# The first output pair's weight sums four units behind their fetch, and other cuts of the last stores, in a hybrid decoder layer

## The chip, the cores and the metric

The kernel runs on one core of one Trainium2 chip. The metric is the device time of one execution in microseconds (us). Three runs of the kernel before took 766.54, 766.78 and 766.79 us; the median is 766.78. Engines are named as in the profile: PE is TensorE with its matmuls, PEld its weight loads, DVE is VectorE, ACT ScalarE, POOL GpSimd, SP SyncE. PE, DVE and ACT each work through their own instructions in the order in which the built program lists them; SP, ACT and POOL also issue the transfers between device memory and on-chip memory.

## The reference

One decoder layer on 256 tokens (two token tiles of 128) of width 2048, in float32. A normed input goes through one wide projection. Two token mixers (a gated delta rule and a block attention, 8 heads of 128 each) give `oa` and `ob`; the end of the layer is:

```python
u_a = oa @ w_branch_a
u_b = ob @ w_branch_b
merged = jax.nn.sigmoid(gate_a) * u_a + jax.nn.sigmoid(gate_b) * u_b
y = merged @ w_out
out = x + rms_norm(y, post_norm_w)
```

`gate_a` and `gate_b` are 2048 columns each of the wide projection. The change touches the product with `w_out`, and the store of `out`.

## The kernel before

**Products in halves.** A float32 operand is split into a high part (cast on ACT, L241) and a low part (the difference, on DVE, L242), and a product is the sum of high by high, high by low and low by high. The tiles are named hi_x and lo_x for a product x. For every weight tile of 128 x 1024 there is thus one ACT cast and one DVE difference, and PE's second matmul of a group needs the low part. `proj_n` does this for a column block of 512: it loads four blocks of 128 rows at a time (raw, three buffers) and splits them in two pieces; lo_gb_1_1 is the low part of the second piece (u = 1) of the second load (kb = 1) of a gate_b block.

**Seven products instead of eight.** The branch products and half of the output product take column blocks in pairs, and multiply 2 x 2 blocks with seven products (`seven`). Three weight tiles tq[0], tq[1], tq[2] for that are fetched by POOL (`fetch`, L776) and added up on DVE (`weight_sums`, L784): first tq[0] += tq[2], in two halves of 128 x 1024, then tq[1] += tq[0], in two halves. After the first two sums POOL issues a fetch that accumulates into tq[2] (L787). `prepare` does the fetch and queues the sums; it is called four times, the last time for the first output pair, column blocks 0 and 1 of w_out. The sums' results are named tq_y there.

**Order of the work.** The program is written out as a stream of matmuls. After each group of six (in a projection with two token tiles) `tick` advances several queues of generators by half a unit; a generator says with `yield n` after how many units it wants to go on. `T_WAIT` has the units that each of the four `weight_sums` waits behind its `prepare`; within it, each half sum is followed by one unit. The instructions of matmuls and of the sums keep their program order; other instructions of an engine are placed by the framework's scheduler when the program is built.

Around the last `prepare` the program does: `merge` of merged column blocks 0 and 1 (transposes on PE, then L1256 to L1271 on ACT and DVE: the transposed blocks mT, the block sums sum_tt, sum_tw, sum_tv, sum_lo for the seven products), `branch(2)` (its weighting is L1168 to L1171 and L1219 to L1220 on DVE), gate_b's column block 3 (a_gb, hi_gb, lo_gb), and then the seven products of the first output pair (a_y, with a_ub of branch block 3 between them).

**The end.** `last` multiplies the last column blocks per token tile; `weigh` squares on ACT (L1316) and multiplies by the norm's weights on DVE (L1317); `finish` takes the root, the reciprocal (L1332), and scales and adds x in five column pieces on DVE (L1336), each stored by its own transfer (L1340): the first token tile's on SP, the last one's on SP and ACT in turn. The last instructions of all engines stand at L1436.

Of the kernel before, what the change touches and what calls it, by code (L numbers as in the profile page):

```python
# [15 lines left out]
P = 128  # L16
# [8 lines left out]
PGT_WAIT = 0.5  # L25
D_WAIT = 7
SC_WAIT = 4
T_WAIT = (5, 4, 4, 7)
L_WAIT = 5
LC_WAIT = 3.5  # L30
INV = (0.6, 2)
# [59 lines left out]
def hybrid_layer(  # L91
# [15 lines left out]
    nc = tc.nc  # L107
    B, S, D = x.shape
# [8 lines left out]
    of = out.rearrange("b s d -> (b s) d")  # L117
# [64 lines left out]
    for c in range(KT // 2):  # L182

        for t in range(NT):
            cs = slice(c * 256, (c + 1) * 256)
# [592 lines left out]
    def weight_sums(tq, w, c, wait):  # L778

        yield wait  # L780
        for o, a in ((0, 2), (1, 0)):
            for u in range(2):
                us = slice(2 * u, 2 * u + 2)
                pin(nc.vector.tensor_tensor(tq[o][:, us], tq[o][:, us], tq[a][:, us], op=ALU.add))  # L784
                yield 1
            if o == 0:
                nc.gpsimd.dma_start(tq[2], block(w, c, 1, 1), accum_op=ALU.add)  # L787
        formed.append(True)

    def prepare(tq, w, c, order):  # L790

        fetch(tq, w, c, order)
        formed.clear()
        sq.add(weight_sums(tq, w, c, T_WAIT[len(tqs)]))
        tqs.append(tq)
# [512 lines left out]
    yw = [big.tile([P, D], F32, tag=f"z{1 - t}", name=f"yw_{t}") for t in range(NT)]  # L1308
# [20 lines left out]
    def finish(t, rb):  # L1329
        rs = wk.tile([P, 1], F32, tag="rstd", name=f"rs_{t}")  # L1330
        pin(nc.scalar.activation(rs, ssy[t][:, 3:4], AF.Sqrt, bias=rb, scale=1.0 / D))
        pin(nc.vector.reciprocal(rs, rs))  # L1332
        for i, (c0, c1) in enumerate(((0, 256), (256, 768), (768, 1280), (1280, 1792), (1792, D))):
            cs = slice(c0, c1)
            pin(
                nc.vector.scalar_tensor_tensor(  # L1336
                    yw[t][:, cs], yw[t][:, cs], rs, hx[:, t, cs], op0=ALU.mult, op1=ALU.add
                )
            )
            (nc.sync if t == 0 or i % 2 == 0 else nc.scalar).dma_start(of[t * P : (t + 1) * P, cs], yw[t][:, cs])  # L1340

    def rest(c, h, pts):

# [60 lines left out]
    last(0, c12, 0, 512)  # L1404
    weigh(3, 0, c12)
    finish(0, rbs[0])
    last(1, c22[:, :256], 0, 256)
    weigh(3, 1, c22[:, :256], 0, 0, 256)
    rb = so_far(1, rbs[1])
    last(1, c22b[:, 256:], 256, 256)  # L1410
    weigh(3, 1, c22b[:, 256:], 3, 256, 256)
    finish(1, rb)


# [26 lines left out]
```

## Time and profile before

| | |
|---|---|
| profiled execution | 766.79 us, its span 765.1 us |
| PEld, ACT, POOL busy | 646.3, 452.7, 52.0 us |
| HBM read and written | 162.72 MB and 3.15 MB, mean 217 GB/s over the span |
| granted TensorE clock, mean over the span | 0.997 |
| sums L784 of the first output pair on DVE | four of 1.22 us, first start 646.0, last 653.4 us |
| the last token tile's stores, from issue to landing | 1.9 to 2.3 us each |

A row of a timeline has the start in us from the span's start, the duration, the engine, the line, the operation and its tiles; a bracket at its end gives the idle time before it and what ended that. Durations of consecutive instructions on one engine overlap a little, so that the distance of two starts, not the duration, says what one more instruction costs. The clock is that granted to TensorE, 1.00 at full speed.

### The profile page before, as it was taken

Reading aid. Unit: us, or ns where it says so; the run is one execution under the profiler, and the core shown is the slowest. Engines: PE = TensorE matmul, PEld = TensorE weight load, DVE = VectorE, ACT = ScalarE, POOL = GpSimd, SP = SyncE. Lnnn points to the kernel's source line nnn. Section 1 sums busy time; section 2 is a strip of 40 time slices with the busy share of each in tenths; the row PEclk is TensorE's granted clock in tenths of the full one; section 3 lists DMA queues with packets and bytes.
Section 4 is the critical chain, followed back from the end, with each engine's and each line's share of the span. In section 5 each row is a group of like instructions: output and inputs, shape, how many; then the busy total and the mean of one; then the engine's idle time right before and its main releaser. Section 6 shows DMA issues by size and latency. Waiting matters only on the chain.

```text
span 765.1 us, 10514 instructions
## 1 busy us (share of the span) xinstructions
PE 755.9 (99%) x3941; PEld 646.3 (84%) x3941; DVE 583.2 (76%) x944; ACT 452.7 (59%) x684; POOL 52.0 (7%) x78
## 2 busy tenths in 40 slices
PE   9999999999999999999999999999999999999996
PEld 8998988899888888888899888787888887888885
DVE  6877669885977898775457876678797778789764
ACT  6776666657655654554556475656556656565751
POOL 4000001112000000003001000101000100100000
PEclk9999999999999999999999999999999999999998
DMA  9585676458555557568437756798979775997972
GB/s 307 177 260 197 194 212 173 137 163 229 185 200 177 189 186 217 171 187 205 127 108 274 209 166 214 250 328 245 334 216 326 221 274 174 338 286 216 270 257 111
DMA packets 100665, 166.56 MB, mean 218 GB/s; under 512 B 3589, under 2 KB 49286, under 8 KB 100102
## 3 DMA queue, kind: packets, MB, share of 16 engines
q1 hardware_dynamic: 89526, 134.93, 53.9%
q0 software_dynamic: 10768, 30.42, 15.4%
q8 instruction: 31, 0.51, 0.3%
q10 hardware_dynamic: 320, 0.53, 0.2%
q14 instruction: 20, 0.16, 0.1%
HBM read 162.72 MB, written 3.15 MB: 217 GB/s over the span
## 4 chain that ended last, share of the span: by engine, by line
PE 94%; DVE 3%; ACT 2%; issue 0%; DVEq 0%
PE a_ga L163 11%; PE a_gb L163 10%; PE a_y L163 9%; PE a_ub L163 6%; PE a_zg L163 6%; PE a_mq L163 6%; PE a_v L163 6%; PE a_mk L163 6%; PE a_k L163 6%; PE a_zm L163 6%; PE a_mv L163 6%; PE a_q L163 4%; PE a_ua L163 4%; PE s L163 1%; PE ms L163 1%; PE po L163 1%
## 5 line engine op out<-in xcount | busy, mean ns | idle before, releaser
L163 PE MATMUL a_ga<-hi_ga,hT 128*128 128x512 f32 x256 | 82.1, 394 | 0.0
L163 PE MATMUL a_gb<-hi_gb,hT 128*128 128x512 f32 x256 | 81.0, 391 | 0.0
L163 PEld LDWEIGHTS a_gb<-hi_gb,hT 128*128 128x128 f32 x256 | 48.0, 188 | 10.5
L163 PEld LDWEIGHTS a_ga<-hi_ga,hT 128*128 128x128 f32 x256 | 48.1, 188 | 10.0
L242 DVE TENSOR_TENSOR lo_ga<-raw_ga,hi_ga 128x1024 fp32r<-128x1024 f32 x32 | 39.1, 1224 | 20.2 <-ACT hi_ga L241 19.8
L241 ACT CAST hi_ga<-raw_ga 128x1024 fp32r<-128x1024 f32 x32 | 33.8, 1055 | 30.8 <-PE a_ga L163 17.5
L163 PE MATMUL a_gb<-lo_gb,hT 128*128 128x512 f32 x128 | 50.4, 394 | 0.5 <-DVE lo_gb L242 0.4
L163 PE MATMUL a_ga<-lo_ga,hT 128*128 128x512 f32 x128 | 50.0, 391 | 0.1
L241 ACT CAST hi_gb<-raw_gb 128x1024 fp32r<-128x1024 f32 x32 | 33.5, 1052 | 25.6 <-PE a_gb L163 14.4
L242 DVE TENSOR_TENSOR lo_gb<-raw_gb,hi_gb 128x1024 fp32r<-128x1024 f32 x32 | 39.1, 1223 | 10.9 <-ACT hi_gb L241 10.6
L163 PE MATMUL a_zg<-hi_zg,hT 128*128 128x348 f32 (+1 forms) x192 | 47.1, 322 | 0.0
L163 PE MATMUL a_mq<-hT,hi_mq 128*128 128x512 f32 x128 | 47.0, 408 | 0.0
L163 PE MATMUL a_mk<-hT,hi_mk 128*128 128x512 f32 x128 | 46.2, 402 | 0.0
L163 PE MATMUL a_q<-hT,hi_q 128*128 128x512 f32 x128 | 45.9, 398 | 0.0
L163 PE MATMUL a_v<-hT,hi_v 128*128 128x512 f32 x128 | 45.3, 399 | 0.0
L163 PE MATMUL a_zm<-hi_zm,hT 128*128 128x512 f32 x128 | 40.5, 392 | 0.0
L163 PE MATMUL a_k<-hT,hi_k 128*128 128x512 f32 x128 | 40.5, 398 | 0.0
L163 PE MATMUL a_mv<-hi_mv,hT 128*128 128x512 f32 x128 | 40.1, 391 | 0.0
L163 PE MATMUL a_v<-hT,lo_v 128*128 128x256 f32 x128 | 35.9, 281 | 0.0
L163 PE MATMUL a_q<-hT,lo_q 128*128 128x256 f32 x128 | 35.9, 280 | 0.0
L163 PE MATMUL a_mq<-hT,lo_mq 128*128 128x256 f32 x128 | 35.9, 280 | 0.0
L163 PE MATMUL a_mk<-hT,lo_mk 128*128 128x256 f32 x128 | 35.8, 280 | 0.0
(459 smaller groups left out, 2043.6 us busy)
## 6 DMA issues: line engine op xcount, KB each, us to landing
raw_ga<-in_w_in_dram SPq DMA_DIRECT2D x16, 1024.0 KB, 5.1
raw_gb<-in_w_in_dram SPq DMA_DIRECT2D x16, 1024.0 KB, 5.7
raw_y<-in_w_out_dram SPq DMA_DIRECT2D x14, 1024.0 KB, 6.2
raw_q<-in_w_in_dram SPq DMA_DIRECT2D x8, 1024.0 KB, 5.6
raw_mv<-in_w_in_dram SPq DMA_DIRECT2D x8, 1024.0 KB, 5.2
raw_v<-in_w_in_dram SPq DMA_DIRECT2D x8, 1024.0 KB, 5.8
raw_zm<-in_w_in_dram SPq DMA_DIRECT2D x8, 1024.0 KB, 5.1
raw_mq<-in_w_in_dram SPq DMA_DIRECT2D x8, 1024.0 KB, 5.7
```

Of the source, the lines that this page charges most:

```text
L163: return pin(nc.tensor.matmul(*args, **kwargs))
L241: nc.scalar.copy(hi, raw)
L242: nc.vector.tensor_tensor(lo, raw, hi.bitcast(F32), op=ALU.subtract)
```

## The change

```diff
-T_WAIT = (5, 4, 4, 7)
+T_WAIT = (5, 4, 4, 4)
...
+        begin = 0
-        for i, (c0, c1) in enumerate(((0, 256), (256, 768), (768, 1280), (1280, 1792), (1792, D))):
+        for i, (c0, c1) in enumerate(((0, 128), (128, 640), (640, 1216), (1216, 1792), (1792, D))):
             cs = slice(c0, c1)
...
-            (nc.sync if t == 0 or i % 2 == 0 else nc.scalar).dma_start(of[t * P : (t + 1) * P, cs], yw[t][:, cs])
+
+            if t == 1 or i in (2, 4):
+                cs = slice(begin, c1)
+                begin = c1
+                (nc.scalar if t == 1 and i % 2 else nc.sync).dma_start(of[t * P : (t + 1) * P, cs], yw[t][:, cs])
```

The weight sums of the first output pair wait four units behind their fetch instead of seven. In `finish` the five column pieces are 128, 512, 576, 576 and 256 wide instead of 256, 512, 512, 512 and 256. The first token tile (t = 0) is stored in two transfers, columns 0 to 1216 and 1216 to 2048; the last one (t = 1) still in five, one for each piece.

In the built program the DVE order around the sums becomes (from L1267 on; before, the same instructions without the four sums stood there in the same order, with the sums ahead of lo_gb_1_1, lo_gb_2_0, lo_gb_2_1 and lo_gb_3_0):

```
L1267, L784 tq[0] first half, L784 tq[0] second half, L1168, L1271 sum_tw,
L784 tq[1] first half, L1171 twice, L1271 sum_tv, L784 tq[1] second half,
L242 lo_gb_1_1, L1271 sum_lo, L242 lo_gb_2_0, lo_gb_2_1, lo_gb_3_0, lo_gb_3_1
```

## The prediction

> **What bounds the kernel now.** I read the page first: busy shares, then the chain that ended last.
>
> ```profile
> span 765.1 us, 10514 instructions
> PE 755.9 (99%) x3941; PEld 646.3 (84%) x3941; DVE 583.2 (76%) x944; ACT 452.7 (59%) x684; POOL 52.0 (7%) x78
> ...
> PE 94%; DVE 3%; ACT 2%; issue 0%; DVEq 0%
> ```
>
> PE is busy for 755.9 of 765.1 us and is 94% of the chain. What it has to do is the time, so only two things can move the end: a new PE wait, or work after PE's last matmul. So I asked next for every PE wait behind the start (columns: who waited for whom, us in total, times, longest).
>
> ```profile
> PE a_gb L163 <- DVE lo_gb L242: 0.4, 1, 0.4
> ```
>
> There is one, 0.4 us, and it lies in the stretch that the change touches. The timeline of PE and then of DVE shows it (start, duration, engine, line, output<-input, count, idle before).
>
> ```profile
> 648.38 0.50 PE L163 MATMUL a_gb<-lo_gb,hT 128*128 128x512 f32 x1 [0.36 <-DVE lo_gb L242]
> ...
> 651.25 0.50 PE L163 MATMUL a_gb<-lo_gb,hT 128*128 128x512 f32 x1
> ```
>
> ```profile
> 637.62 1.23 DVE L242 TENSOR_TENSOR lo_gb<-raw_gb,hi_gb 128x1024 fp32r<-128x1024 f32 x1 [1.00 <-ACT hi_gb L241]
> ...
> 642.36 0.69 DVE L1267 TENSOR_TENSOR gb<-mt,gb 128x512 f32<-128x512 f32 x1
> 642.96 0.68 DVE L1168 TENSOR_TENSOR gb<-gb,a_ub 128x512 f32<-128x512 f32 x1
> 643.56 0.69 DVE L1271 TENSOR_TENSOR sum_tw<-gb,sum_tw 128x512 fp32r<-128x512 f32 x1
> 644.16 1.29 DVE L1171 TENSOR_TENSOR ga<-ga,gb 128x512 f32<-128x512 f32 x2
> 645.36 0.69 DVE L1271 TENSOR_TENSOR sum_tv<-gb,sum_tv 128x512 fp32r<-128x512 f32 x1
> 645.97 1.22 DVE L784 TENSOR_TENSOR tq_y<-tq_y,tq_y 128x1024 f32<-128x1024 f32 x1
> 647.10 1.22 DVE L242 TENSOR_TENSOR lo_gb<-raw_gb,hi_gb 128x1024 fp32r<-128x1024 f32 x1
> ...
> 648.84 1.23 DVE L784 TENSOR_TENSOR tq_y<-tq_y,tq_y 128x1024 f32<-128x1024 f32 x1
> 649.98 1.23 DVE L242 TENSOR_TENSOR lo_gb<-raw_gb,hi_gb 128x1024 fp32r<-128x1024 f32 x1
> ```
>
> The L784 rows are the first two of four weight sums of the first output pair; the other two follow, with one lo_gb in between and one ahead. The lo_gb at 647.10 is lo_gb_1_1, the low half for the second pair of row blocks of gate column block 3's second load; it ends at 648.32, and PE starts on it 0.06 us later. DVE has no idle bracket from 637.62 on. The windows view says the same (window, length, then busy time of PE, PEld, DVE, ACT, POOL, the granted clock, the DMA share and GB/s):
>
> ```profile
> 638.00:648.30 10.30, 10.02 (x44) 7.87 (x42) 10.30 (x16) 5.92 (x9) 0.00 (x0) 1.00 0.46 172
> 648.00:757.65 109.65, 109.29 (x508) 90.45 (x507) 84.83 (x92) 62.89 (x80) 7.30 (x7) 1.00 0.80 248
> ```
>
> For the ten us before this wait DVE is the full engine, with 10.30 of 10.30, and lo_gb_1_1 is already late. Behind it PE is busy for 109.29 of 109.65 us, the missing 0.36 being that wait: PE has no idle time later in which a delay could be made up.
>
> **Part 1: the sums.** The built program's DVE order is changed in one stretch. Before, one sum stood ahead of lo_gb_1_1 and three behind it (each ahead of one of the next three lo_gb). Now all four stand ahead: two right behind L1267, one behind sum_tw, one behind sum_tv. PE's, ACT's and POOL's own orders are unchanged. DVE issues in order, so three more sums go in front of lo_gb_1_1. A sum occupies 1.22 us but the next instruction starts sooner: 645.97 to 647.10 and 648.84 to 649.98 give 1.13 to 1.14, so the three cost 3 x 1.135 = 3.40 us. From 642.36 on: sums at 642.96 and 644.09, L1168 at 645.23, sum_tw 645.83, sum 646.43, L1171 647.56, sum_tv 648.76, the last sum 649.37, lo_gb_1_1 from 650.50 to 651.72. PE can start on it at 651.78. It runs out of work at 648.02 (648.38 - 0.36) and now stands for 3.76 us instead of 0.36: **+3.40 us**.
>
> Could the sums themselves wait, and add to it? Their operands come by POOL's fetches:
>
> ```profile
> 621.97 0.77 POOL L776 DMA_DIRECT2D tq_y<-in_w_out_dram  x1 [13.89 <-DVE ga L1220]
> ...
> 650.37 1.31 POOL L787 DMA_DIRECT2D tq_y<-in_w_out_dram  x1 [12.56 <-DVE tq_y L784]
> ```
>
> ```profile
> DMA to landing us min/median/max: 5.4/8.3/12.5
> ```
>
> (The second row is the landing time of all eight tq_y transfers.) The last of the three fetches is issued at 621.97; even with the longest, 12.5 us from the issue's end at 622.74, it is there by 635.2, 7.8 us ahead of the first sum at 642.96. No wait is added.
>
> What is late next. Queued behind the sums on DVE are sum_lo, at 651.64 (wanted by the fourth sum product, tens of us later), lo_gb_2_0 at 652.24 to 653.47, then lo_gb_2_1 to 654.60. PE reached the second pair's lo 2.87 us after the first's (648.38 to 651.25), so it wants lo_gb_2_0 at 654.65 and the next about 657.5: 1.2 and 2.9 us to spare, no second stall. ACT casts keep waiting for PE's release of their buffers and move with it. On POOL the accumulating fetch L787 waits for the first two sums alone, and goes from 650.37 to about 645.4. On SP the loads wait for the buffers that these lo_gb release:
>
> ```profile
> 648.39 0.37 SPq L827 DMA_DIRECT2D raw_y<-in_w_out_dram  x1
> 653.50 3.78 SPq L827 DMA_DIRECT2D raw_ub<-in_w_branch_b_dram  x2
> ```
>
> ```profile
> 646.00:648.00 2.00, 2.00 (x9) 1.00 0.00 0
> ```
>
> ```profile
> 648.38 13.93 PE a_gb L163 x59
> ```
>
> raw_y goes to 651.8 and the first raw_ub to 654.7. The last row, of the chain, is the cover: 13.93 us of gate matmuls between the stall and PE's first use of raw_y, so that raw_y has 13.9 us from issue to use, as before; raw_ub's use moves 3.4 and its issue 1.2, a gain of 2.2. With a usual 8.3 us to landing and some 2.4 for two more DVE steps of 1.22 (the cast on ACT is no longer), raw_y has 3 us to spare; with 12.5 it would be a us late and cost that. The earlier L787 falls where the DMA engines moved nothing (646 to 648), away from these loads, which makes such a landing less likely. I cost all of this at nothing.
>
> **Part 2: the stores.** The first token tile's five stores on SP become two (columns 0 to 1216, 1216 to 2048); the last tile's pieces become 128, 512, 576, 576, 256 columns, SP and ACT in turn as before. DVE does the same elements in the same five instructions per tile.
>
> ```profile
> L1336 DVE SCALAR_TENSOR_TENSOR yw<-yw,rs,hx 128x512 f32<-128x512 f32 x6 | 4.1, 745 | 0.0
> ...
> L1336 DVE SCALAR_TENSOR_TENSOR yw<-yw,rs,hx 128x256 f32<-128x256 f32 x4 | 1.9, 482 | 0.1
> ```
>
> ```profile
> 758.72 2.87 DVE L1336 SCALAR_TENSOR_TENSOR yw<-yw,rs,hx 128x256 f32<-128x256 f32 x5
> ...
> 761.62 0.33 SPq L1340 DMA_DIRECT2D out_dram<-yw  x1
> ```
>
> 745 against 482 ns for 256 columns more is 1.03 ns a column; 128 fewer in front make the first two pieces ready 0.13 us sooner, the third 0.06 sooner, and the fourth and the last, the same 256 columns, are ready as before, at 761.59 in the time of the profile shown. The last store's issue, at 761.62, does not move. What its data find in front of them does:
>
> ```profile
> 760.60:760.80 0.20, 0.00 (x0) 0.52 0.15 61
> 760.80:761.00 0.20, 0.00 (x0) 0.50 0.91 358
> ...
> 763.20:763.40 0.20, 0.00 (x0) 0.50 0.26 82
> ```
>
> (PE alone this time; then clock, DMA share, GB/s.) From 760.8 to 763.25 the DMA engines are full with the last four pieces, 896 KB (917 thousand bytes) in 2.45 us, 375 GB/s. Now the last four are 960 KB, 2.62 us, and begin 0.13 us sooner: 763.29, **+0.04 us**. Bounds: the stores land within these times, so a last piece with nothing in front of it would gain 0.4; the other way I allow the same.
>
> ```profile
> DMA to landing us min/median/max: 1.9/2.1/2.3
> ```
>
> The first tile's two stores, 1 MB at 375 GB/s, start about 0.8 us behind their pieces' end (755.2 and 756.4) and are out by 758.9, a us before the last tile's first piece moves: nothing.
>
> **Sum.** 765.1 + 3.40 + 0.04 = 768.5 us of span; the profiled execution took 766.79 us for its span of 765.1, so 1.69 lies around it, and the median of the three runs is 766.78, the same: **770.2 us**.
>
> **Rivals.** *A, the clock falls in the stall.* PE would stand for 3.76 us, longer than anywhere in this kernel, and its granted clock does fall in idle time:
>
> ```profile
> 754.61 3.04 PE L163 MATMUL a_y22b<-keep,mT 128*128 128x256 f32 x24
> ...
> 760.40:760.60 0.20, 0.00 (x0) 1.00 0.38 123
> ```
>
> PE ends at 757.65, and the clock is halved at the start of the slice from 760.60, near 760.61 by its mean of 0.52, 2.96 us later. If that delay were the same each time, it would be halved at 650.98, 0.8 us before PE goes on. How long it would stay so, the start shows:
>
> ```profile
> 1.14 2.93 PE L163 MATMUL warm<-ones 128*128 128x128 f32 x12 [1.14 <-DVE epst L197]
> ...
> 4.21 1.11 PE L166 MATMUL hTp<-ident,x 128*128 128x128 f32 x4
> 5.12 1.61 PE L163 MATMUL warm<-ones 128*128 128x128 f32 x8
> 6.51 1.17 PE L163 MATMUL a_k<-hT,hi_k 128*128 128x512 f32 x4
> 7.51 0.60 PE L166 MATMUL hTp<-ident,x 128*128 128x128 f32 x4
> ```
>
> The same four transposes take 1.11 us at 4.21 and 0.60 at 7.51; the eight matmuls from 5.12 to 6.51 go from 0.21 us apart to 0.11 after five of them (5 x 0.21 + 3 x 0.11 = 1.38), near 6.2: PE ran at half rate for some 5 us, losing 2.5. At the other end, if it is noticed as fast as idleness was, 2.96 us at half rate lose 1.5. I take 1.5, since a dense stream of 512 columns resumes here, not short matmuls: 771.7, at most 772.7. For it: 3.76 is over 2.96. Against: that is one fall, and 0.8 us of margin is little if the moment varies from run to run. The Trainium skill ("TensorE: Matmul & The Clock Gate", Part 1, The HAM clock gate) says that activity is judged in free-running windows of about 3.4 us, one idle window halving the clock and one busy window restoring it; by that an idle gap of 3.76 us holds a whole window only for some positions, and a fall would lose half of 3.4, 1.7 us, an estimate from that page: 771.9. The trace agrees that idleness halves the clock, at 2.96 us even before that page's 3.4.
>
> *B, the wait goes instead of growing.* With the sums out from between the lo_gb of this gate, the 0.36 us wait could vanish: 766.5, not slower. Its place is lo_gb_1_1, its price -0.36 + 0.04, and it decides if DVE has 3.4 us to spare ahead of it. The 10.30 of 10.30 us speaks against it; only the 1.00 us that DVE waited for hi_gb at 637.62 lies ahead, on the far side of L1267, where no sum was put.
>
> *C, the sums do not take that place on the chip*, the text's four units making no difference: 766.8. The instruction order of the build is against it.
>
> **How the numbers follow.** The forecast has 0.56, A 0.38, B 0.03, C 0.02; 0.01 is kept for a gain that no row here explains. The forecast's own range, with the store's 0.4 either way, is 769.8 to 770.6. The range given runs from 769.7 to 772.4: it holds A but its longest half-rate time, and leaves out B, C and about a tenth of the rest. A measurement of this kernel tells 0.2%, 1.5 us, from no change: slower is above 768.3. Forecast and A are, by all their bounds: 0.94 slower. B and C lie within 0.2%: 0.05. Faster: 0.01.
>
> **What would show it.** Right: four L784 rows on DVE between 642.9 and 650.6, lo_gb_1_1 near 650.5, a PE wait on lo_gb of 3.7 to 3.8 us at 648.0 and no other beyond 0.1; L787 near 645.4; the granted clock 1.00 in 650 to 656; PE's end near 761.05; the last store 3.4 us later. A: a clock of 0.5 behind the wait, and matmuls of 128x512 twice as far apart for 3 us or more. Wrong: DVE idle time ahead of lo_gb_1_1, a wait within the sums on their fetch, a second PE wait on a later lo, or a tail from PE's end to the span's end that differs from today's 7.45 us by over 0.4.

## The result, and the profile after

The changed kernel took 772.15 us (median of six runs, 771.17 to 772.73) against 766.86 (six runs, 766.54 to 767.21): ratio 1.0067, 95% interval 1.0054 to 1.0080, slower by 5.3 us. It lies in the range of the prediction, 1.95 us above its figure and 0.25 below the upper end; three of the six executions (772.55, 772.57, 772.73) lie above the range. It is 0.45 above the 771.7 that rival A gave. The profiled execution took 772.55 us with a span of 770.85 (to two decimals in the trace; 765.08 before).

All PE waits that the profile after lists (columns as before):

```profile
PE a_gb L163 <- DVE lo_gb L242: 3.8, 1, 3.8
PE warm L163 <- DVE epst L197: 1.1, 1, 1.1
```

The timeline of DVE and of PE after, in the stretch of the change:

```profile
642.60 0.69 DVE L1267 TENSOR_TENSOR gb<-mt,gb 128x512 f32<-128x512 f32 x1
643.21 2.36 DVE L784 TENSOR_TENSOR tq_y<-tq_y,tq_y 128x1024 f32<-128x1024 f32 x2
...
646.67 1.22 DVE L784 TENSOR_TENSOR tq_y<-tq_y,tq_y 128x1024 f32<-128x1024 f32 x1
...
649.61 1.22 DVE L784 TENSOR_TENSOR tq_y<-tq_y,tq_y 128x1024 f32<-128x1024 f32 x1
650.75 1.22 DVE L242 TENSOR_TENSOR lo_gb<-raw_gb,hi_gb 128x1024 fp32r<-128x1024 f32 x1
```

```profile
652.03 0.79 PE L163 MATMUL a_gb<-lo_gb,hT 128*128 128x512 f32 x1 [3.77 <-DVE lo_gb L242]
652.62 1.05 PE L163 MATMUL a_gb<-hi_gb,hT 128*128 128x512 f32 x2
653.47 0.63 PE L163 MATMUL a_gb<-lo_gb,hT 128*128 128x512 f32 x1
653.90 1.06 PE L163 MATMUL a_gb<-hi_gb,hT 128*128 128x512 f32 x2
654.75 0.63 PE L163 MATMUL a_gb<-lo_gb,hT 128*128 128x512 f32 x1
...
668.41 0.39 PE L163 MATMUL a_y<-lo_yp,mT 128*128 128x512 f32 x1
...
760.65 3.04 PE L163 MATMUL a_y22b<-keep,mT 128*128 128x256 f32 x24
```

Against the rows before, everything up to L1267 stands 0.24 us later in this execution, as earlier parts already did. lo_gb_1_1 starts at 650.75 where 647.10 was, and PE takes it up at 652.03 where 648.38 was: 3.65, of which 0.24 is that offset and 3.41 the three sums. Then PE is slow: three matmuls of 512 columns take 1.28 us (653.47 to 654.75), about 0.69 before. The windows view (window, length, PE's busy time with the number of matmuls, clock, DMA share, GB/s) shows why:

```profile
650.00:650.50 0.50, 0.00 (x0) 1.00 1.13 209
650.50:651.00 0.50, 0.00 (x0) 0.61 1.07 197
...
656.50:657.00 0.50, 0.50 (x3) 0.50 0.73 262
657.00:657.50 0.50, 0.50 (x3) 0.57 1.08 418
657.50:658.00 0.50, 0.50 (x4) 1.00 1.03 397
```

The granted clock is halved while PE stands, at 650.61 (a mean of 0.61 over half a us is 0.11 us at 1 and the rest at 0.5), and comes back at 657.43, 5.40 us after PE went on. From the wait's end to the same matmul on lo_yp PE takes 16.38 us (652.03 to 668.41), and 13.99 before (648.38 to 662.37, below): the half rate cost 2.39. PE ends at 763.69, 6.04 later, which is 0.24 + 3.41 + 2.39. The span is 5.77 longer, so the tail behind PE is 0.27 shorter, 7.16 us for 7.43. (With the spans rounded to 0.1 us these are 7.11 and 7.45; the 0.34 in the expectations below is their difference.)

### The profile page after: what moved, and what is told of

Its sections match the earlier page's. It is cut to its first block, busy times and chain, and to the rows that moved or that the text cites. A ratio compares the mean times of both kernels' runs of the same rounds, so it can differ in the third digit from the quotient of the medians.

```text
span 770.8 us, 10508 instructions
## 1 busy us (share of the span) xinstructions
PE 758.4 (98%) x3941; PEld 648.5 (84%) x3941; DVE 583.3 (76%) x944; ACT 452.8 (59%) x684; POOL 52.0 (7%) x78
## 4 chain that ended last, share of the span: by engine, by line
PE 93%; DVE 3%; ACT 2%; issue 1%; DVEq 0%
PE a_ga L163 11%; PE a_gb L163 11%; PE a_y L163 9%; PE a_ub L163 6%; PE a_zg L163 6%; PE a_mq L163 6%; PE a_k L163 6%; PE a_v L163 6%; PE a_mk L163 6%; PE a_zm L163 6%; PE a_mv L163 5%; PE a_q L163 4%; PE a_ua L163 4%; PE s L163 1%; PE ms L163 1%; PE po L163 1%
## 5 line engine op out<-in xcount | busy, mean ns | idle before, releaser
L163 PE MATMUL a_gb<-hi_gb,hT 128*128 128x512 f32 x256 | 82.7, 399 | 0.0
```

The source lines that it names most:

```text
L163: return pin(nc.tensor.matmul(*args, **kwargs))
```

## The experiments

Four kernels ran on one chip, where the kernel before took 767.08 us (21 runs), and three on another, where it took 767.16 (21 runs). Ratios are to those runs.

### The sums alone

The kernel before with `T_WAIT = (5, 4, 4, 4)`, and its own stores.

> Only the sums are moved (four units); the stores are those of the kernel before. Theory (wait plus halved clock): a PE wait on lo_gb of 3.7 to 3.8 us, a granted clock of 0.5 behind it for 3 to 7 us, and the tail of the kernel before, 7.45 us from PE's end to the span's end: 771.4 to 773.1 us, 0.35 above the changed kernel for the same length of half clock. Rival (the stores share in the loss): 770.5 or less.

Measured: 772.32 us (four runs, 771.83 to 773.17), ratio 1.0068, interval 1.0054 to 1.0082. The span of the profiled execution is 770.12, and PE's last row ends at 762.68 (759.64 + 3.04), so the tail is 7.44 us. The PE wait and the clock:

```profile
651.95 0.50 PE L163 MATMUL a_gb<-lo_gb,hT 128*128 128x512 f32 x1 [3.76 <-DVE lo_gb L242]
```

```profile
652.50:653.00 0.50, 0.50 (x3) 0.76 1.16 213
...
656.00:656.50 0.50, 0.50 (x3) 0.83 0.90 340
```

The sums alone bring the whole loss. In this execution the clock fell at 652.76, when PE was already working again for 0.8 us, and was back at 656.17, 3.41 us later. From the wait's end PE takes 15.45 us to the matmul on lo_yp (651.95 to 667.40), so that the half rate cost 1.46 here; in the changed kernel's profile, where it lasted from 650.61 to 657.43, twice 3.41, it cost 2.39.

### The stores alone

The changed kernel with `T_WAIT = (5, 4, 4, 7)`.

> Only the stores are cut differently; the sums stay seven units behind. Theory (the tail became 0.34 us shorter): PE's end to the span's end 7.1 us, against 7.45 before; 766.5 us, ratio 0.9995. Rival (the shorter tail of the changed kernel was that one execution's): tail 7.4 to 7.5, 766.9 us.

Measured: 766.72 us (eleven runs, 766.34 to 767.13), ratio 0.9995, interval 0.9986 to 1.0004: by the times alone not told from no change. The profiled execution has the shorter tail: PE ends at 757.88 and the span at 765.03, 7.15 us. The same holds in every profile: 7.15 to 7.17 us in the six kernels with two stores for the first tile, 7.43 and 7.44 in the two with five. What shortened it, the experiment with three stores asks.

### The same late sums, with PE kept busy

```diff
+FILL = 15
                         mm(pts[t], sh, hi[:, kk, :], start=(k == 0), stop=False)
+                        if name == "gb3" and (k, t) == (6, 0):
+                            fill = aux_tile("fill")
+                            for _ in range(FILL):
+                                mm(fill, hT[:, 0, 0:P], hT[:, 0, :], start=True, stop=True)
                         mm(pts[t], sh, lo[:, kk, :], start=False, stop=False)
```

> The changed kernel with 15 matmuls of 128x512 into a spare PSUM bank between the first matmul of lo_gb_1_1's group and the one that waits; their result is not used. DVE's, ACT's, POOL's and SP's orders are those of the changed kernel, and lo_gb_1_1 comes as late. Theory (the wait costs 3.41 us, idleness costs the rest by the clock): 15 x 0.23 = 3.45 us of the gap are filled, a wait of 0.2 to 0.4 is left, the clock stays at 1.00 up to the end, 769.9 us (766.9 + 3.41 - 0.34). Rival (the half rate comes from something else than idleness): 0.5 clock again, 771.5 to 772.7.

Measured: 770.14 us (four runs, 769.84 to 770.40), ratio 1.0038, interval 1.0025 to 1.0052. The timeline of PE (lines are one further down in this kernel), and one window over the stretch:

```profile
648.44 3.56 PE L164 MATMUL fill<-hT 128*128 128x512 f32 x15
652.37 0.50 PE L164 MATMUL a_gb<-lo_gb,hT 128*128 128x512 f32 x1 [0.37 <-DVE lo_gb L243]
```

```profile
645.00:664.00 19.00, 18.63 (x82) 1.00 0.78 221
```

lo_gb_1_1 is as late as in the changed kernel, PE does nothing useful until then, and the clock stays at 1.00. The time is 3.06 us over before, where 3.41 - 0.27 gives 3.14. The 2.2 us by which the changed kernel's loss is larger (5.29 against 3.06) are thus the price of PE's idleness itself, by the clock; the lateness alone is the other part.

### Fewer sums ahead: five and six units

> The changed kernel with five units: three sums ahead of lo_gb_1_1 instead of four. Theory: a PE wait of 2.63 us (0.36 + 2 x 1.135), 2.27 us over before less 0.34 for the tail: 769.0 us with the clock at 1.00. A gap of 2.6 us leaves at least 0.8 us of work in any stretch of 3.41 us; a stretch with 1.06 us of modelled work let the clock fall in the changed kernel, so it may fall here in some executions: 770 to 771.5 then. Rival (a fall needs a gap longer than 3 us): no execution above 769.6.

Measured: 770.37 us (770.45, 770.30, 768.29, 770.44), ratio 1.0036, interval 1.0022 to 1.0049.

```profile
650.87 0.50 PE L163 MATMUL a_gb<-lo_gb,hT 128*128 128x512 f32 x1 [2.62 <-DVE lo_gb L242]
```

```profile
651.50:652.00 0.50, 0.50 (x4) 0.80 1.13 209
...
655.00:655.50 0.50, 0.50 (x3) 0.79 1.03 389
```

The wait is the 2.6 us expected, and the rival is out: a fall does not need more than 3 us. In the profiled execution the clock fell at 651.80 and was back at 655.21. The mean granted clock over the span is 0.995 in three of the four executions, and 0.997, that of the kernel before, in the one of 768.29. That one has no profile; its time and its clock say that the clock did not fall in it.

> The changed kernel with six units: two sums ahead of lo_gb_1_1. Theory: a PE wait of 1.5 us, 1.135 over before, less 0.34: 767.9 us, clock 1.00 in every execution, as any stretch of 3.41 us has at least 1.8 us of work. Rival (even this lets the clock fall): 769 or more in some executions.

Measured: 767.96 us (ten runs, 767.32 to 768.27), ratio 1.0010, interval 1.0001 to 1.0019. The wait is 1.49 us in its profile and the clock stands at 1.00 until behind PE's end; no execution is above 768.3, and the mean clock is 0.997 to 0.999 in all ten. The sum with the tail of 0.27, 767.16 + 1.135 - 0.27 = 768.03, is met. By the wait that PE had, and with a fall told from the time where there is no profile: 3.77 us, a fall in all ten executions of the two kernels (none under 771.1); 2.62, in three of four; 1.49, in none of ten.

### Nine units: two lo_gb ahead of the sums

> The changed kernel with nine units for the sums: lo_gb_1_1 and lo_gb_2_0 both ahead of the first sum on DVE, the sums ahead of lo_gb_2_1, lo_gb_3_0, lo_gb_3_1 and lo_yp_0. Theory: no PE wait on lo_gb at all (0.36 us less than before) and the shorter tail (0.34 less): 766.2 us, ratio 0.9991. Rival (a wait comes up at a later lo or at the first output product, whose sums are later by two units): 766.5 to 768.

Measured: 765.75 us (eleven runs, 765.14 to 766.18), ratio 0.9981, interval 0.9972 to 0.9990. Behind the start's first matmul its profile lists one PE wait, 0.7 us on the first projection (hi_k), and none on lo_gb. This version is faster than both kernels, and by more than was expected: 1.33 us, not 0.9. Two rows of PE before, and two of this kernel, show the difference:

```profile
647.18 0.39 PE L163 MATMUL a_gb<-lo_gb,hT 128*128 128x512 f32 x1
...
662.37 0.39 PE L163 MATMUL a_y<-lo_yp,mT 128*128 128x512 f32 x1
```

```profile
647.20 0.39 PE L163 MATMUL a_gb<-lo_gb,hT 128*128 128x512 f32 x1
...
661.58 0.39 PE L163 MATMUL a_y<-lo_yp,mT 128*128 128x512 f32 x1
```

The same matmuls take 15.19 us before and 14.38 here. The late lo_gb of before, for which its profile gives a wait of 0.36 us, thus cost 0.81, a gain of 0.81 + 0.27 = 1.08 with the shorter tail; the other 0.25 is within the spread of the runs.

### Three stores for the first token tile

```diff
-            if t == 1 or i in (2, 4):
+            if t == 1 or i in (1, 2, 4):
```

> The stores-only kernel with the first token tile stored in three transfers (columns 0 to 640, 640 to 1216, 1216 to 2048) instead of two; pieces and the last tile's stores the same. The program hands eight completion semaphores around among the transfers, so that the last store's is now the first of the eight (the one that the x load had), not the last. Theory (the tail got shorter because SyncE's closing checks came to the last store's semaphore at their end, with none left to do behind it): with seven checks left behind the last store the tail from PE's end to the span's end is again 7.4 to 7.5 us, or more, as before with five stores; 767.0 us. Rival (fewer or larger stores, or the 128-column first piece, shortened the tail): 7.1 to 7.2, 766.7 us.

Measured: 767.17 us (eleven runs, 766.93 to 767.42), ratio 1.0001, interval 0.9992 to 1.0010. PE's last row ends at 757.74, the span at 765.32: a tail of 7.58 us. SyncE's waits at the end and its events behind 764.05 us, first of the stores-only kernel, then of this one:

```profile
SPq L1441 <- DMA out_dram<-yw: 1.4, 3, 0.5
...
L1441 SPq EVENT_SEMAPHORE  x3: 17/17/28, 764.1 to 765.0; - x3
```

```profile
SPq L1441 <- DMA out_dram<-yw: 1.8, 1, 1.8
...
L1441 SPq EVENT_SEMAPHORE  x9: 17/28/28, 764.1 to 765.3; - x9
```

Both kernels have the same pieces and the same last stores. With two stores SyncE waits three times, for one store after the other; the three events left are the check of the last store, which had been waiting, and two of the closing handshake. With three stores it waits once, 1.8 us, at the first semaphore, for the last store; behind that check (it lies just ahead of the window) come the checks of the seven others and the handshake: nine events. In the kernel before that number was seven, so five checks. Checks behind the last store's and tails go together: none and 7.15 us, five and 7.43, seven and 7.58, some 0.06 us for each check. So the shorter tail is the place of the last store's semaphore in the closing order. The width of the pieces is out as its reason, since these two kernels have the same, and fewer stores by themselves are as well: three have a longer tail than five. The order of the tails rests on the profiles; the times of these two kernels, 0.9995 and 1.0001, have intervals that overlap.

## Why the prediction was right, and where not

**The new wait was right.** Three sums by 1.135 us were to add 3.40 us to the wait on lo_gb_1_1, 3.76 in all; they added 3.41, and it is 3.77. No sum waited for its fetch and there is no second PE wait; L787 went to 645.86, where 645.4 and the offset of 0.24 give 645.64.

**Which case would come was wrong.** "PE runs on at full rate" was given 0.56 and rival A 0.38; every execution was A (771.17 us or more), so that the forecast's own range, 769.8 to 770.6, missed, and the median lies in the stated range because that was drawn wide enough for A. The step that failed is the reading of the one fall that the profile of before had: 2.96 us behind PE's end was taken for about the idleness that a fall needs, with 3.76 only a little over it. The profiles of the nine kernels have that fall behind PE's end too, and it comes after anything from 2.14 us (nine units) to 5.26 us (three stores). What the falls and rises have in common is a grid: within one execution they stand whole multiples of 3.41 us apart. In the changed kernel's profile 650.61, 657.43 and 766.66 are 2 x 3.41 and 32 x 3.413 apart, and the fall and rise of the sums alone and of five units are 3.41 apart. With each execution cut into stretches of 3.41 us by its own grid, PE's busy time in a stretch sorts them:

| stretch | PE busy, us of 3.41 | clock behind it |
|---|---|---|
| changed kernel, 647.20 to 650.61 (the wait) | 1.06 | halved |
| sums alone, 649.35 to 652.76 (the wait) | 0.81 | halved |
| five units, 648.39 to 651.80 (the wait) | 0.93 | halved |
| before, 757.20 to 760.61 (PE's end) | 0.45 | halved |
| nine units, 755.59 to 759.00 (PE's end) | 1.26 | halved |
| three stores, 756.18 to 759.59 (PE's end) | 1.55 | full |
| six units, 757.47 to 760.88 (PE's end) | 1.68 | full |
| stores alone, 756.07 to 759.48 (PE's end) | 1.81 | full |

Two kernels that stand next to each other in this table, nine units and then three stores (windows view as before):

```profile
755.59:759.00 3.41, 1.26 (x11) 1.00 0.67 275
759.00:759.40 0.40, 0.00 (x0) 0.50 0.50 154
```

```profile
756.18:759.59 3.41, 1.55 (x13) 1.00 0.58 231
759.59:763.00 3.41, 0.00 (x0) 1.00 0.72 271
763.00:763.40 0.40, 0.00 (x0) 0.50 0.88 308
```

With 1.26 us of work the clock falls at the stretch's end; with 1.55 it stays, though PE has stopped, until a whole stretch without work has passed. What counts in these profiles is thus how much PE worked in a stretch, not how long it had stood. So the tail of before, with 0.45 us of work, was an easy case. A wait of 3.76 us leaves 1.53 us or less in one of the stretches that it touches, even where the grid cuts it in half. An estimate from these numbers, with a limit anywhere between 1.26 and 1.55 us and every place of the grid equally likely: a wait of 3.76 us lets the clock fall in five of six executions or more (ten of ten did), one of 2.62 in a half to two thirds (three of four did), and one of 1.49, which leaves 1.92 us of work, in none (none of ten did). The Trainium skill ("TensorE: Matmul & The Clock Gate", Part 1, The HAM clock gate) has free-running windows of about 3.4 us, and the trace agrees in that, with 3.413; the table in the section "Why this matters for your kernels" warns of idle gaps above about 3 us, and here a gap of 2.62 us sufficed in three executions of four, so the measured number decides.

**The price of the fall** was given as 1.5 us, at most 2.5. It is 1.2 to 2.7 in the six executions (their times less 766.86 + 3.41 - 0.27 = 770.00), in two groups: 1.17, 1.45 and 1.76 with a mean clock of 0.995 or 0.996, and 2.55, 2.57 and 2.73 with 0.993. The profiled execution is of the second group, and its half rate lasts for two stretches: after a fall with PE still standing, the next stretch has too little work to bring the clock back (1.99 us from 652.03 to 654.02 did not). Where PE is at work again from the fall on, as with the sums alone and with five units, one stretch of 3.41 us does, for the 2.96 of the prediction, and 1.5 us was the right price (1.46 in the profile of the sums alone). The term was too small where, as in that profile, the clock falls while PE still stands.

**The stores** were given +0.04, with 0.4 either way, and brought -0.27. Their data were as forecast: the DMA engines run empty 5.61 us behind PE's end before (763.26) and 5.65 after (some 769.34, by the shares of these slices):

```profile
769.20:769.40 0.20, 0.00 (x0) 0.50 0.66 226
769.40:769.60 0.20, 0.00 (x0) 0.50 0.01 0
```

The gain is SyncE's checks behind the last store, which the sum did not have as a term.

**Rivals B and C fell.** DVE had nothing to spare, and the sums ran where the build put them. The wait that B spoke of can be taken away, but by moving the sums behind lo_gb, two units further back, not ahead.

**Left open** is where between 1.26 and 1.55 us of work in a stretch the limit lies, and how much work brings the clock back (1.99 us did not, 3.41 did). That the executions with a mean clock of 0.993 all had two stretches at half rate is read from one profile and from their times.

## What to carry to other kernels

On a kernel bound by TensorE, ask of every helper instruction moved earlier which operand it now stands in front of: where VectorE has no idle time and that operand is already late, its distance to the next start (1.135 us here, not its duration) goes into TensorE's time in full. Then ask whether the stall starves the clock: here 3.41 us more of waiting cost about 5.6, and 1.13 more no more than itself. Filling a stall with matmuls whose result is not used keeps the rate, but the order that has no stall is better: 765.75 against 770.14 us.

## What was not expected of the hardware

A late lo_gb whose TensorE wait is shown as 0.36 us cost 0.81. Its matmul starts 0.50 us later than in the kernel with nine units (648.38 for 647.88 at the same place), and three matmuls from there take 0.80 us for 0.68. The next lo_gb, lo_gb_2_0, has no wait listed, yet costs 0.13 as well: it ends at 651.21 on DVE, the matmul on it starts at 651.25, and three take 0.81. And the place of the last transfer's semaphore among SyncE's eight closing checks moves the end of the kernel by up to 0.4 us (tails of 7.15, 7.43 and 7.58 us).
